# The rest of a block (merge, recurrence, outputs) asked for two steps later within the next block

## The chip, the cores and the metric

The kernel runs on one core of a Trainium2 chip. The metric is the device time of one execution in microseconds (us). The core's engines are TensorE (PE, with its weight loads PEld), VectorE (DVE), ScalarE (ACT), GpSimd (POOL) and SyncE (SP, which here issues the DMAs). Each engine works through a queue of its own in order, and the engines wait for each other by semaphores.

## The reference

One inference step of a hybrid layer over 4096 prompt rows and 32 sample rows of width 1024:

```
h    = RMSNorm_pre(x);  proj = h @ w_in
y_a  = B_a * conv3(C_a * X_a) * silu(Z_a)                  # group A, 512 channels
q,k,v = silu(conv4(qkv)); q,k L2-normalised                # group B, 4 heads x 128
S_t  = exp(g_t) (I - beta_t k_t k_t^T) S_{t-1} + beta_t k_t v_t^T ;  o_t = q_t^T S_t / sqrt(128)
y_g  = RMSNorm_head(o) * silu(Z_g)
y    = x + RMSNorm_post(concat(y_a, y_g) @ w_out)
```

The recurrence of group B is computed by chunks: within a chunk a triangular system is inverted, and only the state S goes from chunk to chunk. The kernel takes chunks of 128 rows.

## The kernel before

The work has three stages. Stage 1 does group B for 16 blocks of 256 rows (two chunks each, c = 0 and 1); stage 2 does group A; stage 3 multiplies with w_out and norms. The change lies in stage 1.

Within stage 1 the loop over blocks (L767) goes through eight steps `si` (L746): four pairs of q and k columns, two pairs of v columns, two pairs of gate columns z. Each step multiplies one pair of column tiles with the block (`proj`, L382: 48 matmuls of 128x256 f16, written as hi and lo halves, L388 to L390) and convolves or gates the result. In the built program the result tile of block 7 is `pj7_c4` (first step), then `pj7_c6`, `c0`, `c2`, `c8`, `c10`, `z0`, `z2`. Between the steps stand:

- `xprep` (step 2) and `gates` (step 3) for the block that follows, and `decays` after its last step. `gates` makes small matmuls (tile `ggate`, L286 and L288), a chain of small DVE and ACT operations (L290 to L321) and the sums over it (tile `gcs`, L326 to L330);
- `stage1` (steps 4 and 5, one chunk each; 3 and 4 in the last two blocks): transposes (L426), the products of k with k and q (L442), DVE masks them (L443, L444), SP writes the 32x32 diagonal parts to DRAM (L450);
- `subst` (step 5): SP reads those parts back (L485), DVE scales (L490), and POOL inverts the 32x32 triangles in 62 dependent operations after one larger one (L495, L499, L500); SP writes the result (tile `lt`, L503) and reads it in another layout (tile `Tc`, L510);
- `finish` for the block before (L748), which is what the change touches. Its part 0 is `merge` (L516): from the 32x32 inverses the 128x128 ones, by many matmuls of 32x32 and 64x64 (tile `m`, L546 to L560, the first of which read `Tc`). Part 1 is `rec_a` of chunk 0 (tiles `rt`, `rk`, `rq`, `rv`, `rS`, L574 to L596, ending in the new state S at L599), part 2 is `rec_b` of chunk 0 (tiles `oo` and `om`, L611 to L632) and `rec_a` of chunk 1, part 3 is `rec_b` of chunk 1;
- `prep_a`, at some steps: preparation of the weights of group A (tiles `gL`, `gu`, `hl`).

The written order is not yet the order on the engines. The framework's scheduler (switched on at L1249) puts each engine's queue in an order of its own: of what stands ready in its model it prefers what was written earlier. The queues are then fixed, and the chip runs each of them in order. The scheduler also has to respect the buffers: M, at and kd (L431, L437) have four buffers for two chunks a block, v and zg two, U (L513) and Tc (L504) one, PSUM bank `m` one, banks `r` two.

After the loop, `finish` is called once more for the last block (L830).

Of the kernel before, what the change touches and what calls it, by code (L numbers as in the profile page):

```python
# [31 lines left out]
BIT = 1 << 23  # L32
NXT = 5
SG = 0
LS = 2
XPE = 256
AH = 1
# [13 lines left out]
def hybrid_kernel(  # L51
# [513 lines left out]
    def rec_a(b, c):  # L565

        C = b["C"]
        nm = f"{b['id']}_{c}"
        sl = slice(c * C, (c + 1) * C)
        qk, v, U, kd = b["qk"], b["v"], b["U"][c], b["kd"][c]  # L570
        S = state[b["s"]]
        vt = bank("r", [P, NH, P], f"t{nm}")[:C]
        for h in range(NH):
            T.transpose(vt[:, h], v[:, h, sl], ident)  # L574
        R = tl([P, NH, P], F32, "R", 2, nm)[:C]
        for h in range(NH):
            A.activation(R[:, h], vt[:, h], AF.Copy, scale=b["br"][:, c, h:h + 1])
        pk = bank("r", [P, NH, P], f"k{nm}")[:C]
        for h in range(NH):
            T.matmul(pk[:, h], qk[:, h, 0, sl], S[:, h], start=True, stop=True)  # L580
        for h in range(NH):
            V.scalar_tensor_tensor(R[:, h], pk[:, h], b["nbe"][:, c, h:h + 1], R[:, h], ALU.mult, ALU.add)
        pq = bank("r", [P, NH, P], f"q{nm}")[:C]
        for h in range(NH):
            T.matmul(pq[:, h], qk[:, h, 1, sl], S[:, h], start=True, stop=True)
        o = tl([P, NH, P], F32, "o", 2, nm)[:C]
        for h in range(NH):
            A.activation(o[:, h], pq[:, h], AF.Copy, scale=b["e1"][:, c, h:h + 1])
        pv = bank("r", [P, NH, P], f"v{nm}")[:C]
        for h in range(NH):  # L590
            T.matmul(pv[:, h], U[:C, h, :C], R[:, h], start=True, stop=True)
        vn = tl([P, NH, P], F32, "vn", 1, nm)[:C]
        A.activation(vn, pv, AF.Copy)
        pS = bank("r", [P, NH, P], f"S{nm}")
        for h in range(NH):
            T.matmul(pS[:, h], kd[:, h], vn[:, h], start=True, stop=True)  # L596
        Sn = tl([P, NH, P], F32, "S", 3, nm)
        for h in range(NH):
            V.scalar_tensor_tensor(Sn[:, h], S[:, h], b["egl"][:, c, h:h + 1], pS[:, h], ALU.mult, ALU.add)  # L599
        state[b["s"]] = Sn  # L600
        b["rec"] = (o, vn)

    def rec_b(b, c):

        C = b["C"]
        nm = f"{b['id']}_{c}"
        sl = slice(c * C, (c + 1) * C)
        o, vn = b["rec"]
        po = bank("o", [P, NH, P], f"o{nm}")[:C]
        for h in range(NH):  # L610
            T.matmul(po[:, h], b["at"][c][:, h, :C], vn[:, h], start=True, stop=True)  # L611
        V.tensor_tensor(o, o, po, ALU.add)
        so = tl([P, 3, NH], F32, "so", 2, nm)[:C]
        jk = b["at"][c]
        for h in range(NH):
            A.activation(jk[:, h], o[:, h], AF.Square, accum_out=so[:, 0, h:h + 1])
        f = so[:, 1]
        V.tensor_tensor(so[:, 0], so[:, 0], b["c2"][:, c], ALU.mult)
        V.tensor_scalar(so[:, 0], so[:, 0], EPS, None, ALU.add)
        rsqrt(so[:, 0], f, so[:, 2])  # L620
        V.tensor_tensor(f, f, b["cc"][:, c], ALU.mult)
        V.tensor_tensor(o, o, bc(f, 2, P), ALU.mult)
        pm = bank("o", [P, NH, P], f"m{nm}")[:, :, :C]
        for h in range(NH):
            T.transpose(pm[:, h], o[:, h], ident[:C, :C])
        mg = b["zg"][:, :, sl]
        V.scalar_tensor_tensor(mg, pm, gwc, mg, ALU.mult, ALU.mult)
        if b["s"]:
            dma(mxd_s[:, NH:], mg)
        else:  # L630
            o0 = b["o"] + c * C
            dma(mxd[o0 // NB2][:, NH:, o0 % NB2:o0 % NB2 + C], mg)  # L632
# [14 lines left out]
    def prep_b(ct):  # L647

        for i, w in enumerate(scaled((ct, ct + 1))):
            hi, lo = W[ct + i] = w_tile(ct + i)  # L650
            A.activation(hi, w, AF.Copy)
            (V if ct + i in VLO else G).tensor_tensor(lo, w, hi, ALU.subtract)  # L652
        if ct < 28:
            c = ct - 16
            V.tensor_tensor(cw[:, :, c:c + 2], cw[:, :, c:c + 2], bc(usc[:, ct:ct + 2], 1, 4), ALU.mult)
# [52 lines left out]
    def out_state(b):  # L708
        dma((ngd_s if b["s"] else ngd_p)[0, 0].rearrange("h k v -> k h v"), state[b["s"]])
# [3 lines left out]
    smp = blocks1[0]  # L713
    groups[SG].insert(0, smp)
    xprep(groups[0][0])
# [6 lines left out]
    prep_b(20)  # L722
    if SG == 0:
        xprep(groups[0][1])
# [22 lines left out]

    def finish(prevs, si):  # L748

        for p in prevs:  # L750
            n = p["nch"]
            if si == 0:
                merge(p)
            elif si == 1:
                rec_a(p, 0)
            elif si == 2:
                rec_b(p, 0)
                if n > 1:
                    rec_a(p, 1)
            elif si == 3:  # L760
                if n > 1:
                    rec_b(p, 1)
                if p["last"]:
                    out_state(p)

    prevs = []
    for gi, grp in enumerate(groups):  # L767
# [11 lines left out]
        for si, (kind, c0) in enumerate(steps):  # L779
# [11 lines left out]
            for b in grp:  # L791
# [5 lines left out]
                else:  # L797
                    h0 = c0 % 4
                    qkv_pair(b, c0, b["qk"][:, h0:h0 + 2, 0 if kind == "k" else 1, :n])
            finish(prevs, si)  # L800
            if si == (2 if gi else 6) and gi + 1 < len(groups):
                for b in groups[gi + 1]:
                    xprep(b)
            s1 = 4 if gi + LS < len(groups) else 3
            if si in (s1, s1 + 1):
# [20 lines left out]
        prevs = grp  # L826
# [1 line left out]
        prep_a()  # L828
    early.close()
    for si in range(4):  # L830
        finish(prevs, si)
    late.close()


# [418 lines left out]
```

## Time and profile before

| | |
|---|---|
| median of 3 runs | 2398.5 us (2389.68 to 2398.57) |
| profiled execution, its own time | 2393.51 us |
| its span, first to last instruction | 2391.8 us |
| mean granted TensorE clock | 0.962 |
| last projection matmul of stage 1 | starts at 1320.27 us |
| PE busy | 2156.4 us, 90% of the span |
| DVE, POOL, ACT busy | 1699.0 (71%), 1195.2 (50%), 992.5 us (41%) |

The span lies 1.7 us below the profiled execution's own time, which lies 5.0 us below the median of the runs. Busy time is the time in which an engine had an instruction of the program in work. Matmuls overlap, so PE's busy share is read together with its idle time and with the granted clock (1.0 is 2.4 GHz, 0.5 is 1.2 GHz; values between are means over both).

### The profile page before, as it was taken

Reading aid. Unit: us, or ns where it says so; the run is one execution under the profiler, and the core shown is the slowest. Engines: PE = TensorE matmul, PEld = TensorE weight load, DVE = VectorE, ACT = ScalarE, POOL = GpSimd, SP = SyncE. Lnnn points to the kernel's source line nnn. Section 1 sums busy time; section 2 is a strip of 40 time slices with the busy share of each in tenths; the row PEclk is TensorE's granted clock in tenths of the full one; section 3 lists DMA queues with packets and bytes.
Section 4 is the critical chain, followed back from the end, with each engine's and each line's share of the span. In section 5 each row is a group of like instructions: output and inputs, shape, how many; then the busy total and the mean of one; then the engine's idle time right before and its main releaser. Section 6 shows DMA issues by size and latency. Waiting matters only on the chain. (4 is left out here: it accounts for less than half of the span.)

```text
span 2391.8 us, 48652 instructions
## 1 busy us (share of the span) xinstructions
PE 2156.4 (90%) x18626; PEld 1706.8 (71%) x18626; DVE 1699.0 (71%) x4666; ACT 992.5 (41%) x2497; POOL 1195.2 (50%) x1581
## 2 busy tenths in 40 slices
PE   3677989899999999999999799899999999999998
PEld 3566877778777777787778678788888887444443
DVE  4886878987689888786777675676575565666763
ACT  4454656565666566555654220222121121433321
POOL 3526246752575644454454740766456611554542
PEclk9888999999999999999989899999999999999999
DMA  6334333534333442244324304311211133443431
GB/s 117 53 93 106 80 75 96 116 82 92 92 100 78 109 112 75 68 91 118 70 72 125 101 24 174 104 66 54 80 59 39 54 100 98 136 150 115 157 115 54
DMA packets 296913, 221.39 MB, mean 93 GB/s; under 512 B 166392, under 2 KB 236856, under 8 KB 296680
## 3 DMA queue, kind: packets, MB, share of 16 engines
q1 hardware_dynamic: 296680, 218.28, 33.5%
q8 instruction: 146, 2.39, 0.4%
q14 instruction: 87, 0.71, 0.1%
HBM read 127.84 MB, written 74.64 MB: 85 GB/s over the span
## 5 line engine op out<-in xcount | busy, mean ns | idle before, releaser
L388 PE MATMUL pj_c<-hhi,w 128*128 128x256 f16 x1536 | 429.3, 280 | 1.2 <-DMA hhi<-xth 1.2
L390 PE MATMUL pj_c<-hhi,w 128*128 128x256 f16 x1536 | 429.7, 280 | 0.0
L389 PE MATMUL pj_c<-hlo,w 128*128 128x256 f16 x1536 | 428.9, 279 | 0.0
L867 PEld LDWEIGHTS <-w_a 128*128 128x128 f16 x2880 | 269.9, 99 | 59.5 <-issue 25.6
L1130 PEld LDWEIGHTS <-opm 128*128 128x128 f16 x1536 | 149.6, 98 | 189.8 <-issue 15.5
L500 POOL TENSOR_TENSOR lt<-lt 128x112 f32<-128x112 f32 (+29 forms) x496 | 250.0, 504 | 38.9
L495 POOL TENSOR_TENSOR la<-la,lt 128x1024 f32<-128x1024 f32 x16 | 38.7, 2421 | 449.9 <-DVE lt L490 270.9
L390 PEld LDWEIGHTS <-w 128*128 128x128 f16 x2176 | 215.5, 100 | 53.2 <-POOL w L652 23.0
L499 POOL TENSOR_TENSOR lt<-la,lt 128x112 f32<-128x112 f32 (+29 forms) x496 | 233.1, 470 | 38.8
L388 PEld LDWEIGHTS <-w 128*128 128x128 f16 x2176 | 215.8, 100 | 34.1 <-issue 2.1
L389 PEld LDWEIGHTS <-w 128*128 128x128 f16 x2176 | 215.7, 100 | 30.7 <-issue 0.5
L405 DVE SCALAR_TENSOR_TENSOR qk<-u,cw,qk 128x256 f32<-128x256 f32 x384 | 214.9, 596 | 9.0 <-ACT qk L403 8.4
L867 PE MATMUL pja<-op,w_a 128*128 128x256 f16 x1536 | 194.5, 276 | 7.0 <-DVE w L881 3.4
L1079 POOL TENSOR_TENSOR mab<-mab 128x1024 bf16<-128x1024 bf16 (+2 forms) x48 | 103.6, 2159 | 130.8 <-ACT mab L1077 128.4
L867 PE MATMUL ga<-op,w_a 128*128 128x256 f16 x1152 | 149.8, 275 | 14.0 <-DVE w L881 8.1
L389 PE MATMUL pj_z<-hlo,w 128*128 128x256 f16 x512 | 144.6, 282 | 0.0
L390 PE MATMUL pj_z<-hhi,w 128*128 128x256 f16 x512 | 144.4, 282 | 0.0
L388 PE MATMUL pj_z<-hhi,w 128*128 128x256 f16 x512 | 144.3, 282 | 0.0
L1130 PE MATMUL pjo<-w_o,opm 128*128 128x512 f16 x528 | 118.2, 379 | 3.8 <-DVE v13y L1154 2.0
L1130 PE MATMUL ro<-w_o,opm 128*128 128x512 f16 x504 | 114.7, 383 | 3.9 <-DVE v7y L1154 2.0
L881 DVE TENSOR_TENSOR w<-pja,w 128x256 f32<-128x256 f32 x168 | 67.4, 420 | 70.6 <-PE pja L867 68.0
L1130 PE MATMUL go<-w_o,opm 128*128 128x512 f16 x504 | 112.7, 379 | 3.9 <-DVE v19y L1154 2.0
(707 smaller groups left out, 4946.5 us busy)
## 6 DMA issues: line engine op xcount, KB each, us to landing
xt<-in_x_prompt_dram SPq DMA_DIRECT2D x32, 512.0 KB
op<-hTd SPq DMA_DIRECT2D x32, 512.0 KB
mx<-mxd SPq DMA_DIRECT2D x16, 1024.0 KB
xtw<-in_w_in_dram SPq DMA_DIRECT2D x28, 512.0 KB
wad<-hl SPq DMA_DIRECT2D x56, 256.0 KB
gB<-gd SPq DMA_DIRECT2D x16, 516.0 KB
hTd<-hhi SPq DMA_DIRECT2D x16, 512.0 KB
hTd<-hlo SPq DMA_DIRECT2D x16, 512.0 KB
```

Source lines behind the costliest of these rows:

```text
L388: T.matmul(pt[:, i, :n], wh[:, k, :], b["hi"][:, k, :n], start=k == 0, stop=False)
L389: T.matmul(pt[:, i, :n], wh[:, k, :], b["lo"][:, k, :n], start=False, stop=False)
L390: T.matmul(pt[:, i, :n], wl[:, k, :], b["hi"][:, k, :n], start=False, stop=k == KT - 1)
L405: V.scalar_tensor_tensor(d, u[:, i, j:j + n], cw[:, j, c0 + i:c0 + i + 1], d, ALU.mult, ALU.add)
L495: E.tensor_tensor(la, la, bc(rl, 1, 32), ALU.mult)
L499: E.tensor_tensor(tm, bc(la[:, j, j + 1:32], 2, w), bc(lt[:, j, 0:w], 1, r), ALU.mult)
L500: last = E.tensor_tensor(lt[:, j + 1:32, 0:w], lt[:, j + 1:32, 0:w], tm, ALU.subtract)
L867: T.matmul(out, lt(x, k), rh(y, k), start=start and k == n == 0, stop=stop and k == 3 and n == 2)
L881: V.tensor_tensor(dst, p, src, ALU.add)
L1079: G.tensor_tensor(ab[:, 0:m], ab[:, 0:m], ab[:, m:2 * m], ALU.add)
L1130: T.matmul(p, mo[:, x, k, t * P:t * P + m], WO[y, k][:, hf * 512:hf * 512 + 512], start=k == i == 0, stop=k == KT - 1 and i == 2)
```

## The change

`finish` subtracts FS = 2 from the step, so that its parts 0 to 3 are asked for at steps 2 to 5 instead of 0 to 3; at the other steps it does nothing. The call after the loop adds 2 again, so that the last block ends as it did.

```diff
 SG = 0
+FS = 2
 LS = 2
...
     def finish(prevs, si):
 
+        si -= FS
         for p in prevs:
             n = p["nch"]
             if si == 0:
                 merge(p)
...
     for si in range(4):
-        finish(prevs, si)
+        finish(prevs, si + FS)
     late.close()
```

Both programs hold the same instructions, as many of each line on each engine; only their order differs. Line numbers of the new program are one higher from L35 on and two higher from L751 on. Three places follow.

PE, where the merge of block 6 starts. Before, this is in the last projection of block 7 (`pj7_z2`):

```order
L388 MATMUL pj7_z2_9716<-hhi7_8033,w30_31_1930 128x256
L389 LDWEIGHTS w30_31_1930
L389 MATMUL pj7_z2_9716<-hlo7_8034,w30_31_1930 128x256
L546 MATMUL m6_8771<-Tc6_8542,M6_0_8328 32x32
L625 MATMUL om5_1_8154<-ident_63,o5_1_8011 128x128 x4
L546 MATMUL m6_8771<-Tc6_8542,M6_0_8328 32x32
L390 LDWEIGHTS w31_31_1931
L390 MATMUL pj7_z2_9716<-hhi7_8033,w31_31_1931 128x256
```

Now it is in `pj7_c10`, two projections earlier, and the gate sums of block 8 (`gcs8`) and the last transposes of block 5 (`om5_1`) stand right in front of it:

```order
L330 LDWEIGHTS g38_9188
L330 MATMUL gcs8_9193<-ctr_76,g38_9188 8x129
L626 MATMUL om5_1_8399<-ident_63,o5_1_8252 128x128 x4
L547 MATMUL m6_8895<-Tc6_8542,M6_0_8295 32x32
L331 MATMUL gcs8_9193<-ident_63,beta8_9181 8x128
L547 MATMUL m6_8895<-Tc6_8542,M6_0_8295 32x32
L427 MATMUL gt07_0_9358<-ident_63,qk7_8698 128x128 x4
L547 MATMUL m6_8895<-Tc6_8542,M6_0_8295 32x32
L389 LDWEIGHTS w20_26_1454
L389 MATMUL pj7_c10_9394<-hhi7_7908,w20_26_1454 128x256
```

So the merge, asked for two steps later in the program, stands earlier in PE's queue than before. From the last product of `stage1` of a block (L442) to the first merge multiply of that block (L546) the queue holds these projection matmuls, by block:

| block | 3 | 4 | 5 | 6 | 7 | 8 | 9 | 10 | 11 | 12 | 13 |
|---|---|---|---|---|---|---|---|---|---|---|---|
| before | 284 | 289 | 328 | 318 | 294 | 284 | 289 | 288 | 328 | 315 | 296 |
| now | 282 | 282 | 288 | 279 | 280 | 289 | 279 | 280 | 289 | 279 | 279 |

Before, the merges of blocks 3, 4, 8, 9 and 10 start in the `c10` projection of the block that follows, those of 5, 6, 7, 11, 12 and 13 in `z0` or `z2`; now all eleven start in `c10`.

DVE, the start of the chain of the gates of block 8. Before, the convolution of block 7 (L405) and an output of block 5 (L627) stand between its links:

```order
L290 COPY g168_9277<-ggate8_9244 128x32
L292 TENSOR_TENSOR gz8_9279<-g168_9277 128x16
L400 COPY hist7_8701<-u7_8_9377 128x6
L293 TENSOR_TENSOR gz8_9279<-gz8_9279,ug_97 128x16
L294 TENSOR_TENSOR gz8_9279<-gz8_9279,dtb_94 128x2x4
L297 TENSOR_SCALAR gex8_9283<-gz8_9279 128x2x4
L405 SCALAR_TENSOR_TENSOR v7_8699<-u7_8_9377,cw_98,v7_8699 128x256
L296 SCALAR_TENSOR_TENSOR gex8_9283<-gz8_9279 128x2x4
L405 SCALAR_TENSOR_TENSOR v7_8699<-u7_8_9377,cw_98,v7_8699 128x256 x2
L302 TENSOR_SCALAR gu8_9287<-gex8_9283 128x16
L405 SCALAR_TENSOR_TENSOR v7_8699<-u7_8_9377,cw_98,v7_8699 128x256
L627 SCALAR_TENSOR_TENSOR zg5_6597<-om5_0_7980,gwc_95,zg5_6597 128x4x128
```

Now the small operations of block 5's last norm (`so5_1`) stand there:

```order
L291 COPY g168_9165<-ggate8_9132 128x32
L399 COPY u7_10_9443<-hist6_7650 128x2x3
L293 TENSOR_TENSOR gz8_9167<-g168_9165 128x16
L294 TENSOR_TENSOR gz8_9167<-gz8_9167,ug_97 128x16
L619 TENSOR_TENSOR so5_1_8379<-so5_1_8379,sm5_7405 128x4
L295 TENSOR_TENSOR gz8_9167<-gz8_9167,dtb_94 128x2x4
L298 TENSOR_SCALAR gex8_9171<-gz8_9167 128x2x4
L620 TENSOR_SCALAR so5_1_8379<-so5_1_8379 128x4
L297 SCALAR_TENSOR_TENSOR gex8_9171<-gz8_9167 128x2x4
L115 TENSOR_SCALAR so5_1_8379<-so5_1_8379 128x4
L116 TENSOR_SCALAR so5_1_8379<-so5_1_8379 128x4
L303 TENSOR_SCALAR gu8_9175<-gex8_9171 128x16
```

The two chains, of the gates and of the norm, now run side by side, and no large operation lies within them there.

SP, where the inverses of block 7 are stored and read back. Before, an output of block 6 (L632) and the gate rows of block 9 (L340, L342) are issued ahead of them:

```order
L632 DMA mxd3_112<-zg6_7649 128x4x128
L340 DMA gd9_10370<-row9_10366 8x129
L342 DMA bd9_10372<-brow9_10368 8x128
L503 DMA ltd7_9623<-lt7_9547 128x256
L510 DMA Tc7_9625<-ltd7_9623 128x4x8 x8
L450 DMA lad8_9786<-M8_0_10462 32x4x32 x4
```

Now the second output of block 6 and the gate rows come behind them:

```order
L504 DMA ltd7_9623<-lt7_9547 128x256
L511 DMA Tc7_9625<-ltd7_9623 128x4x8 x8
L633 DMA mxd3_112<-zg6_7649 128x4x128
L341 DMA gd9_10258<-row9_10254 8x129
L343 DMA bd9_10260<-brow9_10256 8x128
L451 DMA lad8_9786<-M8_0_10429 32x4x32 x4
```

So here the store and the load that feed the merge stand ahead of the DMAs that wait for DVE's gate rows and for the output of block 6.

## Rows read from the trace of the kernel before

**Rows 1.** The page: span, busy time, PE's busy tenths and clock by slices.
```profile
span 2391.8 us, 48652 instructions
PE 2156.4 (90%) x18626; PEld 1706.8 (71%) x18626; DVE 1699.0 (71%) x4666; ACT 992.5 (41%) x2497; POOL 1195.2 (50%) x1581
...
PE   3677989899999999999999799899999999999998
...
PEclk9888999999999999999989899999999999999999
```

**Rows 2.** Timeline of PE, two projection matmuls: start, duration, instruction.
```profile
854.76 0.27 PE L390 MATMUL pj_z<-hhi,w 128*128 128x256 f16 x1
854.87 0.27 PE L388 MATMUL pj_z<-hhi,w 128*128 128x256 f16 x1
```

**Rows 3.** Windows: stretch, length, busy by engine (x), PEclk, DMA share, GB/s.
```profile
407.20:1248.60 841.40, 777.41 (x7226) 658.79 (x7224) 679.46 (x2068) 492.63 (x1316) 457.63 (x825) 0.96 0.37 90
...
563.20:634.60 71.40, 65.41 (x617) 56.44 (x615) 53.71 (x177) 40.77 (x107) 46.22 (x79) 1.00 0.46 108
...
863.50:943.80 80.30, 73.11 (x663) 60.89 (x661) 69.58 (x189) 46.51 (x123) 48.34 (x79) 0.94 0.42 97
...
1019.50:1095.50 76.00, 69.46 (x618) 58.29 (x616) 53.91 (x177) 40.80 (x107) 46.22 (x79) 0.93 0.45 107
1095.50:1170.70 75.20, 69.20 (x651) 59.41 (x649) 61.95 (x197) 46.12 (x126) 34.35 (x68) 1.00 0.30 70
```

**Rows 4.** Waits of PE from 407.2 to 1248.6: total us, times, longest.
```profile
PE m L546 <- DMA Tc<-ltd: 18.5, 12, 2.4
PE rk L580 <- DVE S L599: 9.3, 10, 3.0
PE om L625 <- DVE o L622: 7.8, 11, 1.4
PE gu L206 <- DVE wu L199: 7.1, 4, 2.3
PE gcs L326 <- DVE g L321: 6.8, 5, 2.6
```

**Rows 5.** Windows of two, three, three and three blocks.
```profile
407.20:563.20 156.00, 143.06 (x1333) 120.56 (x1332) 126.60 (x367) 91.83 (x243) 81.32 (x147) 0.96 0.37 84
563.20:786.90 223.70, 207.08 (x1964) 178.12 (x1962) 181.15 (x587) 134.68 (x359) 127.05 (x226) 0.99 0.40 99
786.90:1019.50 232.60, 215.23 (x1996) 180.67 (x1993) 191.78 (x548) 135.38 (x362) 125.87 (x226) 0.95 0.37 90
1019.50:1248.60 229.10, 212.04 (x1942) 179.45 (x1939) 179.94 (x568) 130.73 (x353) 123.38 (x226) 0.95 0.35 85
```

**Rows 6.** Timeline of PE: rS of chunk 0 and rk of chunk 1, block 6.
```profile
738.07 1.06 PE L596 MATMUL rS<-vn,kd 128*128 128x128 f32 x8
...
744.31 0.91 PE L580 MATMUL rk<-S,qk 128*128 128x128 f32 x3 [2.98 <-DVE S L599]
```

**Rows 7.** Timeline of PE: last gate matmul for block 8, its first gate sum.
```profile
678.32 0.34 PE L288 MATMUL ggate<-wg,hlo 128*128 128x8 f16 x8
...
689.11 0.18 PE L326 MATMUL gcs<-g,rev 128*128 128x24 bf16 x1
```

**Rows 8.** Timeline of POOL: first and last operation of the inversions of blocks 12, 13.
```profile
1118.80 2.54 POOL L495 TENSOR_TENSOR la<-la,lt 128x1024 f32<-128x1024 f32 x1 [29.65 <-DVE lt L490]
...
1157.06 0.21 POOL L500 TENSOR_TENSOR lt<-lt 128x8 f32<-128x8 f32 x1
...
1187.60 2.47 POOL L495 TENSOR_TENSOR la<-la,lt 128x1024 f32<-128x1024 f32 x1 [27.57 <-DVE lt L490]
...
1221.02 0.20 POOL L500 TENSOR_TENSOR lt<-lt 128x8 f32<-128x8 f32 x1
```

**Rows 9.** Timeline of PE: the first merge multiply of blocks 12 and 13.
```profile
1160.99 0.24 PE L546 MATMUL m<-Tc,M 32*32 32x32 f32 x2 [1.57 <-DMA Tc<-ltd]
...
1225.03 0.24 PE L546 MATMUL m<-Tc,M 32*32 32x32 f32 x2 [1.77 <-DMA Tc<-ltd]
```

## The prediction, made before the changed kernel was run

> **What bounds the kernel now.** I read the page first [rows 1]. The reader is to see that PE is busy for 90% of a span of 2391.8 us and that its row is at 9 tenths in most slices after the start: PE sets the time. The change lies in stage 1, whose projections end at about 1320 us. A projection matmul starts 0.11 us after the one before it [rows 2], and each block has 8 x 48 = 384 of them, 42 us; with its smaller matmuls a block takes 71 to 80 us [rows 3].
>
> Next come the windows. I take the eleven blocks of the steady state, 4 to 14, from 407.2 to 1248.6 us: each holds the merge and the recurrence of the block before it, 3 to 13. They take 841.4 us, in which PE is idle for 841.4 - 777.4 = 64.0 us at a mean granted clock of 0.96 [rows 3]. If PE is what everything waits for, a clock of 0.96 loses 4% of the stretch, some 34 us. So idle time and clock together, about 98 us, are all that another order of the same work can win here, and there is as much room for a loss.
>
> Last, the list of PE's waits in this stretch [rows 4]. The largest is the merge waiting for Tc: 18.5 us in 12 waits. No wait is longer than 3 us. The rest of a block is late in none of these rows by anything like a step (some 9 us): PE has filled the time with projections already.
>
> **The change, part by part.** It adds and removes no instruction, so the work costs nothing more. What moves is the order, and less of it than two steps: the scheduler had already put the merge where Tc lands in its model, five or more steps into the next block. Asked for later, it now stands in c10 in all eleven blocks, where five of the eleven stood already. Six merges (blocks 5, 6, 7, 11, 12, 13) come one or two projections earlier.
>
> *The wait for Tc, and idle time as a whole.* The old queue has both places, so it prices them itself. Three late merges (5, 6, 7) lie in 563.2 to 786.9: idle 223.70 - 207.08 = 16.6 us. Three early ones (8, 9, 10) in 786.9 to 1019.5: idle 232.60 - 215.23 = 17.4 us. Three late ones again (11, 12, 13) in 1019.5 to 1248.6: 17.1 us [rows 5]. Early against the mean of late: +0.5 us for three, **+1 us** for six. The merge is not earlier than its data allow, because POOL's inversion, which it waits for, hangs on stage1 and not on finish, and its queue keeps its order. From the last product of stage1 to the merge the new queue has 279 to 289 projections; of the early merges before, 284 to 289. So Tc should be waited for as those were, about 2 us each.
>
> *The clock.* The same windows show 0.99 and 0.95 with the late merges, mean 0.97, and 0.95 with the early ones, on a nearly equal number of matmuls (1964, 1942 and 1996) [rows 5]. 0.02 of 229 us is 4.6 us for three merges, 9 us for six. But the windows 563.2 to 634.6 and 1019.5 to 1095.5 hold a queue that repeats after six blocks (617 and 618 matmuls), one at 1.00 in 71.4 us, the other at 0.93 in 76.0 us [rows 3]: the clock moves by as much without a change of order. I take half, **+5 us**, with bounds of 0 and +9.
>
> At this place the Trainium skill speaks against the change: "TensorE: Matmul & The Clock Gate", section "A second HAM failure mode: psum-queue depth-cycling", tells of a kernel whose PE idles briefly and often between groups of matmuls, so that its clock swings between the two levels and throughput goes to that. The trace agrees in kind: no wait here is longer than 3.0 us, and the clock is below 1.0 in every stretch all the same. By the rule alone every merge placed among short waits would be paid for; the sum by it is that of the third rival, 2415 us, against 2402 by the rows.
>
> *The recurrence.* In block 6 rk of chunk 1 stood 4 projections and 18 small gate matmuls behind rS of chunk 0, and waited 2.98 us for the state [rows 6]; in the new queue 18 projections, 2 us, lie between. That wait should go: **-3 us**. The other rk waits (9.3 us in all with this one, [rows 4]) keep their distance of some 19 projections or get more; lower bound -6, upper 0.
>
> *Gates and the last transposes.* These now stand in a row directly ahead of the merge. From the last gate matmul to the first gate sum took 689.11 - 678.66 = 10.4 us in block 7, where PE did not wait for it [rows 7]; the new queue has 69 to 76 projections there, 7.5 to 8.3 us. So PE will come to gcs about 2 us early in each block. I price this at **0**, because the merge right behind it would wait about as long for Tc anyhow: two waits that end at the same time cost one. Without that cover it would be 2.1 us in eleven blocks, 23 us. Bounds 0 and +23.
>
> *The queues of SP and POOL.* On SP the store and load of the inverses go past an output DMA and the gate rows in some blocks. The load starts no earlier for it where POOL is the one waited for: from the end of POOL's last operation to the merge it takes 1160.99 - 1157.27 = 3.7 us in block 12 and 1225.03 - 1221.22 = 3.8 us in block 13 [rows 8, 9], one store and one load with nothing left to take out. The gate rows now wait behind them, but are read only after the block's last step. Cost 0. M, at and kd have four buffers, which hold two blocks; the last part of finish is over before stage1 takes the third: no new wait. The end of stage 1 and the stages behind it keep their order but for a few matmuls: 0.
>
> Sum: 2393.5 us of the profiled execution + 1 + 5 - 3 + 0 = 2396.5 us. The median of the runs lies 5.0 us above that execution, so I forecast **2402 us**, +0.1%. No change that can be measured; about 0.5% (12 us) is what a measurement of this kernel can tell from none.
>
> **The rivals.**
>
> *Faster: Tc arrives before PE does.* POOL's 63 operations took 1157.27 - 1118.80 = 38.5 us in block 12 and 1221.22 - 1187.60 = 33.6 us in block 13 [rows 8], the same operations beside other DVE work. If the new neighbours leave them at 33.6 us everywhere, Tc lands up to 4.9 us earlier, the 18.5 us of waits go [rows 4], and with them perhaps half of the 34 us of clock: -35 us, 2363 us. For it: DVE's large operations lie elsewhere now. Against: block 13 with its 33.6 us still waited 1.77 us [rows 9], and the place of the merge follows the same model.
>
> *Slower: the gate chain becomes the wait that ends last.* It decides from the point where gcs is ready later than Tc. Price 2.1 us in eleven blocks, +23 us: 2422 us with the forecast's other terms near zero. For it: the new distance of 7.5 to 8.3 us lies below the 10.4 us that the chain took in block 7. Against: Tc's wait stands in the same place and covers it.
>
> *Slower: the clock falls at every merge.* The rule of the Trainium skill quoted above, in "TensorE: Matmul & The Clock Gate", points this way. The worst early block ran at 0.94 [rows 3]; eleven blocks at 0.94 instead of 0.96 give 0.02 x 841.4 = +17 us, 2415 us. For it: the two stretches with early merges are at 0.96 and 0.95 [rows 5]. Against: a late one is at 0.95 too, and its worst block at 0.93.
>
> **How the numbers follow.** The forecast 0.54, the faster rival 0.18, the gate chain 0.13, the clock 0.15. The forecast's own range takes the bounds of its terms, -5 to +10 us on the median, 2394 to 2409, and half of the runs' scatter of 9 us to either side: 2389 to 2413. The whole range reaches up past both slower rivals, to 2426, and down into the milder third of the faster one, 2380; below that I leave 0.12, above 0.07. Slower by over 0.5%: 0.13 + 0.15 = 0.28; faster 0.18; within, 0.54.
>
> **What would show it.** In the changed profile: equal counts of instructions; from 407 to 1249 us about the same length of eleven blocks (840 to 850 us); PE idle of 60 to 68 us; waits of m for Tc of 15 to 22 us, gcs up, the rk wait of 3 us gone; a clock of 0.95 to 0.96. The forecast is wrong if the idle time of the stretch moves by more than 10 us or its clock by more than 0.015, and then the line that moved tells which rival came: m with POOL's duration, gcs, or the clock alone.

## The result, and the profile after

The changed kernel takes 2419.92 us (median of 4 runs, 2417.8 to 2426.01), the kernel before 2394.09 us in the same measurement (4 runs, 2389.16 to 2398.57). The ratio is 1.0115, with a 95% interval of 1.0091 to 1.0139: slower by about 26 us. That lies inside the whole range of the prediction (2380 to 2426), but above the forecast's own (2389 to 2413), and on the side of the two slower rivals. The forecast itself, 2402 us and no change that can be measured, missed.

The page of the changed kernel, and the window of the blocks 4 to 14, which now run from 405.5 to 1270.2 us (stretch, length, busy by engine, PEclk, DMA share, GB/s), answer to [rows 1, 3]:

```profile
span 2416.1 us, 48665 instructions
...
PE 2164.4 (90%) x18626; PEld 1713.7 (71%) x18626; DVE 1723.5 (71%) x4666; ACT 990.7 (41%) x2497; POOL 1201.4 (50%) x1581
```
```profile
405.50:1270.20 864.70, 786.68 (x7274) 664.26 (x7273) 698.97 (x2069) 492.58 (x1319) 461.78 (x825) 0.95 0.36 88
```

The reader is to see three things. The eleven blocks take 864.7 us instead of 841.4, so 23.3 of the 24.3 us by which the two profiled spans differ were lost here; the stretch starts 1.7 us earlier than before, and nothing behind stage 1 moved by more than a few us. PE's idle time in it is 864.7 - 786.7 = 78.0 us instead of 64.0. And DVE is busy for 699.0 us instead of 679.5 with one instruction more in the window, and over the whole span for 1723.5 instead of 1699.0 us with 4666 in both: the same work, longer.

PE's waits in this stretch (us in total, times, longest) answer to [rows 4]:

```profile
PE gcs L327 <- DVE g L322: 21.3, 10, 4.9
PE rk L581 <- DVE S L600: 13.2, 11, 2.4
PE rS L597 <- ACT vn L594: 11.2, 9, 1.4
PE om L626 <- DVE o L623: 10.7, 13, 2.3
PE m L547 <- DMA Tc<-ltd: 8.1, 7, 2.8
PE gu L207 <- DVE wu L200: 6.1, 4, 1.7
```

Two further lines of the same view of the kernel before, which did not stand among its rows:

```profile
PE rS L596 <- ACT vn L593: 4.8, 6, 1.2
PE rv L591 <- DVE R L582: 3.9, 5, 1.4
```

The merge's wait for Tc fell from 18.5 to 8.1 us, the wait of the gate sums rose from 6.8 to 21.3, and the waits of the recurrence and the last transposes rose too: rk by 3.9, rS by 6.4, om by 2.9 us; rv's 3.9 us are gone.

The largest single wait shows how it comes. PE at the gate sums in block 7 (start, duration, instruction, idle before it and what ended it; the first line is the last group of gate matmuls), answering to [rows 7]:

```profile
679.68 0.34 PE L289 MATMUL ggate<-wg,hlo 128*128 128x8 f16 x8
...
692.51 0.18 PE L327 MATMUL gcs<-g,rev 128*128 128x24 bf16 x1 [4.94 <-DVE g L322]
```

From the first line to the gate sums 12.8 us pass, 4.94 of them idle. DVE, in the last part of the gate chain at that time:

```profile
686.96 1.08 DVE L312 TENSOR_TENSOR gu<-gu,ru 128x8 f32<-128x8 f32 x1
687.97 0.15 DVE L118 TENSOR_TENSOR so<-so 128x4 f32<-128x4 f32 x1
688.08 1.08 DVE L313 TENSOR_TENSOR gsp<-gsp,gu 128x8 f32<-128x8 f32 x1
689.08 0.15 DVE L119 SCALAR_TENSOR_TENSOR so<-so 128x4 f32<-128x4 f32 x1
689.19 0.17 DVE L314 SCALAR_TENSOR_TENSOR gsp<-gz,gsp 128x8 f32<-128x8 f32 x1
689.27 0.15 DVE L120 SCALAR_TENSOR_TENSOR so<-so 128x4 f32<-128x4 f32 x1
689.39 1.24 DVE L315 TENSOR_TENSOR gsp<-gsp,nea 128x8 f32<-128x8 f32 x1
...
691.28 1.18 DVE L322 TENSOR_TENSOR g<-gsp,g 128x8 bf16<-128x8 f32 x1
```

and POOL, which has finished the inversion and prepares weights of group A:

```profile
685.75 3.39 POOL L676 TENSOR_TENSOR hl<-xtw,hl 128x512 f16<-128x512 f32 x3
689.08 0.31 POOL L492 MEMSET lt<- 128x256 f32 x1
689.35 1.26 POOL L682 TENSOR_TENSOR xtw<-xtw 128x512 f32<-128x512 f32 x1
690.55 0.53 POOL L494 MEMSET lt<- 32x8 f32 x4
691.15 1.28 POOL L684 TENSOR_TENSOR xtw<-xtw,xtw 128x512 f32<-128x512 f32 x1
```

Operations on 8 numbers per partition take 0.15 to 0.17 us, or 1.08 to 1.24 us. The long ones started while POOL ran a 128x512 operation, and ended with it: L315 at 689.39 + 1.24 = 690.63, POOL's L682 at 689.35 + 1.26 = 690.61; L322 at 692.46, POOL's L684 at 692.43. L314, beside POOL's MEMSET, took 0.17. Four such operations make the chain some 4 us longer. In block 8 POOL has no such work at this place, and from the gate matmuls to the gate sums 771.66 - 762.88 = 8.8 us pass:

```profile
762.88 0.34 PE L289 MATMUL ggate<-wg,hlo 128*128 128x8 f16 x8
771.66 0.17 PE L327 MATMUL gcs<-g,rev 128*128 128x24 bf16 x1 [0.77 <-DVE g L322]
```

Over the stretch, the waits of gcs are 1.8 to 4.9 us in the six blocks 4, 6, 7, 9, 10 and 12, where POOL's wide operations lie in the chain, 18.0 us together, and 0.7 to 1.1 us in blocks 5, 8, 11 and 13, where they do not. From the gate matmuls to the gate sums it takes 12.7 to 13.6 us in the six, 8.7 to 8.9 us in the four. Such long operations were no rarer in the gate chains before (22 in the eleven blocks, 23 now). But then PE's queue held 8.7 to 14.6 us of work between the last gate matmul and the first gate sum in the blocks 4 to 13; now it holds 7.5 to 8.7 in the blocks 5 to 13 (an estimate: the operations in between by the order, each at its mean duration in the trace).

### The profile page after: what moved, and what is told of

It reads as the page before. It is cut to its first block, busy times and chain, and to the rows that moved or that the text cites. A ratio compares the mean times of both kernels' runs of the same rounds, so it can differ in the third digit from the quotient of the medians.

```text
span 2416.1 us, 48665 instructions
## 1 busy us (share of the span) xinstructions
PE 2164.4 (90%) x18626; PEld 1713.7 (71%) x18626; DVE 1723.5 (71%) x4666; ACT 990.7 (41%) x2497; POOL 1201.4 (50%) x1581
## 5 line engine op out<-in xcount | busy, mean ns | idle before, releaser
L496 POOL TENSOR_TENSOR la<-la,lt 128x1024 f32<-128x1024 f32 x16 | 38.1, 2380 | 452.3 <-DVE xss L118 281.9
L406 DVE SCALAR_TENSOR_TENSOR qk<-u,cw,qk 128x256 f32<-128x256 f32 x384 | 203.8, 569 | 11.1 <-ACT qk L404 10.3
L898 ACT ACTIVATE op<-tsc 128x512 f16<-128x512 f32 x60 | 37.8, 629 | 191.5 <-POOL tsc L904 116.4
```

Of the source, the lines that this page charges most:

```text
L406: V.scalar_tensor_tensor(d, u[:, i, j:j + n], cw[:, j, c0 + i:c0 + i + 1], d, ALU.mult, ALU.add)
L496: E.tensor_tensor(la, la, bc(rl, 1, 32), ALU.mult)
L898: A.activation(f[:, q, 0, hf], t, AF.Copy)
```

## The experiments

Three theories stood first. *Gate theory*: the loss is the short distance between gate matmuls and gate sums. *Place theory*: merges that all lie in c10 cost by themselves, by short waits and the clock. *Priority theory*: what counts is which parts of `finish` the scheduler sees behind which neighbour. In the built queues, asking later for the last outputs alone (part 3 at step 4 or 5) changes nothing at all; the order of the kernel before comes out again. All times below are medians of the runs of that measurement, with the ratio to the kernel before in it.

**Only the recurrence later** (merge asked for at step 0, rec_a of chunk 0 and the part behind it at step 3, the last outputs at 5).

```diff
+    FIN = (0, 3, 3, 5)   # steps of parts 0 to 3; before: (0, 1, 2, 3)
...
```

(`finish` then does part k at step FIN[k]; that code is left out here.)

> Parts 0 to 3 of finish at steps 0, 3, 3, 5: of the whole change only the first recurrence (part 1) passes xprep; the merge and the outputs stand where they did before gates. In its queue the merge of blocks 3 to 13 starts in c10 in every block, as in the changed kernel, and 69 to 77 projections lie between the last gate matmul and the first gate sum, 7.5 to 8.4 us, as in the changed kernel. Gate theory (PE comes to the gate sum before DVE has finished its chain, pays, and the clock falls behind it): as slow as the changed kernel, 2410 to 2422 us, gcs waits of 18 us or more in all. Place theory (the merge in c10 costs, by its neighbours and the clock): the same time, gcs waits of any size. Priority theory (what costs is that outputs and second recurrence come behind the gates): as before, 2390 to 2400 us.

Measured: 2415.41 us, ratio 1.0082 (1.0052 to 1.0112). Most of the loss, with the merge asked for where it was, and the gate sums wait for 18.9 us: as the gate theory and the place theory expected. The priority theory's 2390 to 2400 us are missed.

**The rest behind the gates** (merge and first recurrence asked for as before, the parts behind them after the gates).

```diff
+    FIN = (0, 1, 4, 5)
...
```

> Parts at steps 0, 1, 4, 5: only the second recurrence and the outputs pass the gates. In its queue every merge of blocks 3 to 13 still starts in c10 or just behind it, but 8 to 14 us of projections (mean 10.5) lie between the last gate matmul and the first gate sum, with 8.4 to 15.6 us before the last transposes. Gate theory: near the kernel before, 2393 to 2406 us, gcs waits of 12 us or less. Place theory: as slow as the changed kernel, 2412 to 2422 us, clock 0.957 or less. Priority theory: as slow as the changed kernel.

Measured: 2432.18 us, ratio 1.0145 (1.011 to 1.0181). Its distance from gates to gate sums is 7.8 to 14.3 us, mostly longer than in the changed kernel, and it is slower. The gate theory's 2393 to 2406 us are missed, and its gate sums wait for 15.7 us where 12 at most were expected. The other two theories have the direction, but too small a loss.

**Gates one step earlier** (in the changed kernel).

```diff
-            if si == (3 if gi else 7) and gi + 1 < len(groups):
+            if si == (2 if gi else 7) and gi + 1 < len(groups):
```

> The changed kernel (FS = 2) with the gates of the block that follows asked for at step 2 instead of 3. In its queue every merge starts in c10 and even 2 us earlier than in the changed kernel, but 9.4 to 14.3 us of projections lie between the last gate matmul and the first gate sum. Gate theory: the loss goes, 2390 to 2402 us, gcs waits of 9 us or less. Place theory: the loss stays, 2412 to 2422 us, clock 0.957 or less. Priority theory: as slow as the changed kernel.

Measured: 2436.41 us, ratio 1.0172 (1.0142 to 1.0203), with a distance of 9.4 to 14.3 us. The slowest of all, where the gate theory expected the loss to go; the gate sums still wait for 14.9 us. Its gate chains have only 5 operations of over 0.9 us from block 4 to 14, against 22 in the kernel before and 23 in the changed one, but the norm's (tile `so`) have 21, against 6 and 2, and PE waits for om for 15.3 us.

**Three steps later instead of two.**

```diff
-FS = 2
+FS = 3
```

> FS = 3. Every merge in c10; 9.3 to 15.7 us of projections before the gate sums, 9 to 11 us before the last transposes. Gate theory: between the two kernels, 2395 to 2408 us, gcs waits of 6 to 14 us. Place theory: 2412 to 2422 us. Priority theory: as slow as the changed kernel or slower.

Measured: 2425.14 us, ratio 1.0124 (1.0095 to 1.0153). The distance is 9.3 to 15.7 us and the gate sums wait for 0.7 us in all, but now the last transposes wait. PE's waits in its blocks 4 to 14:

```profile
PE om L626 <- DVE o L623: 21.3, 10, 3.9
PE m L547 <- DMA Tc<-ltd: 14.4, 10, 3.2
```

The wait of om is again one for a chain of small DVE operations (the norm). So the gate theory fell in its narrow form: the distance of the gates is one of several, and lengthening it moved the wait to another chain. In the two longest of these waits (3.9 us) operations of the gate chain that take 1.1 to 1.2 us stand among those of the norm; in others (3.3 us at 917.48 us) it is the convolution (L406) that stands there. The *contention theory* came out of the first kind: these chains are long where POOL's 128x512 operations run, and PE waits for whichever of them is tight in the queue. Of the four runs only the first speaks against the priority theory, which says nothing of how the time is lost.

**POOL's 128x512 operations left out**, in the old and the new places, with a copy by ACT for the missing half.

```diff
-            G.tensor_tensor(hl[:, 1], src, hl[:, 0], ALU.subtract)
+            A.activation(hl[:, 1], src, AF.Copy)
...
-        G.tensor_tensor(a22, a21, a22, ALU.add)
```

(The other three sums and differences went likewise; the old places are FS = 0.)

> The kernel before, with one part left out: in the preparation of group A's weights, the 128x512 operations of POOL (the low half of each split, and the four sums and differences ahead of it). A copy by ACT takes the place of the low half, so that the DMAs and tiles stay; the weights of group A are then wrong. Contention theory (what the change costs is that the gate chain and the norm chain now lie where POOL runs these operations, beside which small DVE operations take 1.1 instead of 0.16 us): here the gain is small, 2383 to 2394 us, since six of the eleven merges and their chains lie elsewhere. Place theory (a merge in the c10 projection costs by itself, whatever POOL does): 2385 to 2400 us. This run is the base for the next one.

> The changed kernel with the same part left out (POOL's 128x512 operations in the preparation of group A's weights, a copy by ACT in place of the low half). Its queue still has all eleven merges in c10. Contention theory: the small DVE operations of the gate chain are back at 0.16 us, the chain takes 8.5 us in every block, the idle time of PE from block 4 to 14 is 60 to 68 us, and this kernel lies at most 8 us above the same one with the old places (no_pool_prep_before). Place theory: it lies 18 to 30 us above it, as the changed kernel lies above the one before, with idle time still at 75 us or more.

Measured: 2402.85 us with the old places, ratio 1.0034 (1.0014 to 1.0054), and 2404.48 us with the new, 1.0042 (1.0022 to 1.0062): the change now costs 1.6 us instead of 26. No DVE operation of the gate chains took over 0.9 us in either. But the first number missed its range, the idle time of the second is 79.6 us where 60 to 68 were expected, and its gate sums still waited for 14.1 us. From block 4 to 14 of the second, ACT waits for 33.5 us, once for 15.8, until a DMA has stored an earlier part of the weights and freed its buffer (hl has four); in these blocks of the kernel before and of the changed one it never waits for that. What stands behind it in ACT's queue is late, gates and recurrence too, which made this pair a poor test.

**The preparation asked for later**, behind the gate chain of the next block, all work kept, in the old and the new places.

```diff
-            if si == 6 and 1 <= gi <= 13 or si == 2 and gi in (4, 7, 10):
+            if si == 4 and 2 <= gi <= 14:
...
+                        tc.issue_after(groups[gi + 1][-1]["gates_end"]):
```

> The kernel before, all work kept: the preparation of group A's weights is asked for in step 4 of the next block and issued only behind that block's gate chain, so that POOL's 128x512 operations no longer lie beside the gates. Contention theory: gate chain 8.5 us in every block, 2380 to 2394 us. Place theory: no difference from the kernel before, 2390 to 2400 us.

> The same move of the preparation in the changed kernel; it too puts POOL's 128x512 operations behind the gate chain, and the queue then has the merges partly in c10 and partly in z0 (their places change with it). Contention theory: gate chain 8.5 us in every block, idle time 60 to 68 us from block 4 to 14, 2388 to 2402 us. Place theory: the blocks whose merge stays in c10 stay slow, 2405 to 2420 us.

Measured: 2427.05 us, ratio 1.0136 (1.0109 to 1.0163), and 2426.19 us, 1.0138 (1.0104 to 1.0172). Both theories missed. The gate chains had no slow operation any more except in block 14, but POOL's operations now ran beside other ones: in the first kernel PE waited 14.3 us for om and 5.9 us for kd. So PE waited elsewhere instead.

**POOL's operations left out, nothing put in their place** (the DMA stores the high half twice).

```diff
-            G.tensor_tensor(hl[:, 1], src, hl[:, 0], ALU.subtract)
-            dma(wad[i][:, k], hl)
+            dma(wad[i][:, k], bc(hl[:, 0], 1, 2))
...
```

(The four sums and differences went as above.)

> The changed kernel, with POOL's 128x512 operations in the preparation of group A's weights left out, and this time nothing put on ACT in their place: the DMA stores the high half twice. The weights of group A are then wrong. PE's queue keeps the distances of the changed kernel: 7.5 to 8.6 us of work between the last gate matmul and the first gate sum, and every merge in c10. Contention theory: the gate chain is at most 9.5 us long in every block instead of 12.4 to 13.4 us in six of them, the waits of gcs fall from 21.3 to at most 9 us from block 4 to 14, the idle time from 78 to 62 to 70 us, and the time is 2398 to 2410 us. Queue theory (the chain is long because of the other DVE work that stands in it): the gcs waits stay at 17 us or more, and the time at 2412 to 2422 us.

> The same part left out (POOL's 128x512 operations in the preparation of group A's weights, nothing put in their place) with the old places of merge, recurrence and outputs: the partner of the run that took the changed kernel from 1.0115 to 1.0014 of the kernel before. Contention theory (most of what the change costs comes from chains of small DVE operations that now lie beside these operations): without them the old and the new places differ by at most 8 us, so a ratio of 0.998 to 1.005 to the kernel before, 2391 to 2408 us. Place theory (the new places cost about 25 us whatever POOL does, and leaving POOL's work out is worth 21 us in either kernel): a ratio of 0.988 to 0.993, 2367 to 2379 us.

Measured: with the new places 2398.48 us, ratio 1.0014 (0.9995 to 1.0033); with the old 2397.26 us, ratio 1.0007 (0.9991 to 1.0024). So the same removal takes 1.0% off the changed kernel and, on balance, nothing off the kernel before, and without these operations the two places can't be told apart. That is what the contention theory said, and the place theory's 0.988 to 0.993 for the second did not come. The gate chain of block 7 in the first of the two, from the last group of gate matmuls to the gate sums, and one of its operations on DVE, with no wait left:

```profile
690.99 0.34 PE L289 MATMUL ggate<-wg,hlo 128*128 128x8 f16 x8
698.73 0.18 PE L327 MATMUL gcs<-g,rev 128*128 128x24 bf16 x1
```
```profile
697.12 0.17 DVE L315 TENSOR_TENSOR gsp<-gsp,nea 128x8 f32<-128x8 f32 x1
```

7.7 us instead of 12.8, with the same operations, and 0.17 us instead of 1.24. PE's waits in its blocks 4 to 14:

```profile
PE m L547 <- DMA Tc<-ltd: 22.1, 10, 11.7
PE rS L597 <- ACT vn L594: 14.8, 6, 9.8
PE gu L207 <- DVE wu L200: 12.8, 7, 2.3
PE rk L581 <- DVE S L600: 12.3, 7, 7.8
...
PE gcs L327 <- DVE g L322: 1.0, 1, 1.0
```

The wait of gcs went from 21.3 to 1.0 us, as expected; the idle time did not fall to 62 to 70 us, it is 79.4. But 29.4 us of it are three single waits, of m (11.7), rS (9.8) and rk (7.8), longer than any in these blocks of the changed kernel. The last two stand behind ACT, which waits again until a buffer of the weights is free, 20.4 us in all; at rS:

```profile
ACT hl L675 <- DMA wad<-hl: 20.4, 7, 9.1
```
```profile
911.96 0.63 ACT L675 ACTIVATE hl<-xtw 128x512 f16<-128x512 f32 x1 [8.69 <-DMA wad<-hl]
912.50 0.58 ACT L594 ACTIVATE vn<-rv 128x512 f32<-128x512 f32 x1
```

The products rv that this vn reads had ended at 899.9 us. The wait of 11.7 us for Tc at 461.5 us, where the store of the inverses took some 10 us, stands in its partner too (11.64 us at 457.7) and in the kernel with ACT's copies and the old places (11.75 us at 453.1), while no wait for Tc in these blocks is longer than 6.1 us in the ten kernels that keep POOL's operations. So the removal brings waits of its own. Without the three, 50.0 us of idle time are left, and the waits are 10.4 us for m, 5.0 for rS and 4.5 for rk.

**The scaling ahead of the inversion on DVE**, in the old and the new places, all work kept: the one other wide operation of POOL in a block, 128x1024 and 2.4 us.

```diff
-        E.tensor_tensor(la, la, bc(rl, 1, 32), ALU.mult)
+        V.tensor_tensor(la, la, bc(rl, 1, 32), ALU.mult)
```

> The kernel before, all work kept: the 128x1024 multiplication at the head of the inversion, 2.4 us on POOL in each block, is done by DVE. Contention theory, in its strong form (the time that DVE loses beside POOL is what PE waits for): DVE gains more than it gives, about 23 us less lost from block 4 to 14 against some 12 us of work added, and POOL's chain is shorter, so 2375 to 2392 us. Theory of the lucky order (every order other than that of the kernel before costs 8 to 42 us by waits that turn up on other lines, as in all eight other orders so far): 2400 to 2425 us, although DVE loses less.

> The same move of the 128x1024 multiplication to DVE in the changed kernel. Contention theory in its strong form: 2392 to 2410 us. Theory of the lucky order: 2405 to 2430 us, within 8 us of the run with the old places (scaling_on_dve_before), since neither is then the order of the kernel before.

Measured: 2426.92 us, ratio 1.0131 (1.0096 to 1.0166), and 2419.51 us, 1.009 (1.0066 to 1.0113). The contention theory in its strong form fell. Its premise did not hold in the first kernel: DVE is busy for 692.5 us there from block 4 to 14, 13.0 more than before, as much as the work added (11 operations of 1.22 us). In the second it is busy for 691.6, 7.4 less than in the changed kernel, and the time is not clearly below that of the changed kernel (1.009 against 1.0115, with intervals that overlap). The theory of the lucky order has the second and misses the first by 2 us. The first kernel's merges wait for Tc for 37.4 us:

```profile
PE m L547 <- DMA Tc<-ltd: 37.4, 11, 6.1
```

In its queue most merges stand 42 to 44 us of PE's work (an estimate as above) behind the last product of stage1, against 44 to 51 us in the kernel before: it seems that the scheduler counts on an earlier Tc and places them earlier than it comes. No version that keeps all the work beat the kernel before.

**All runs by one account.** Blocks 4 to 14 of each profiled run: length, idle time of PE (length less busy), what the clock took (for each of the eleven blocks its length times 1 less its PEclk, summed), and the rest.

| | ratio | length | idle | clock | rest |
|---|---|---|---|---|---|
| before | 1 | 841.4 | 64.0 | 32.5 | 744.9 |
| changed | 1.0115 | 864.7 | 78.0 | 39.9 | 746.8 |
| only the recurrence later | 1.0082 | 866.5 | 76.3 | 44.0 | 746.2 |
| rest behind the gates | 1.0145 | 879.5 | 91.4 | 42.8 | 745.3 |
| gates one step earlier | 1.0172 | 886.9 | 94.2 | 47.0 | 745.6 |
| three steps later | 1.0124 | 862.2 | 73.9 | 41.8 | 746.5 |
| preparation later, old / new places | 1.0136 / 1.0138 | 857.7 / 855.9 | 76.1 / 76.6 | 36.1 / 35.9 | 745.5 / 743.3 |
| ACT copy, old / new places | 1.0034 / 1.0042 | 852.3 / 861.2 | 75.6 / 79.6 | 35.6 / 40.1 | 741.1 / 741.4 |
| left out, old / new places | 1.0007 / 1.0014 | 849.2 / 855.6 | 76.9 / 79.4 | 31.7 / 34.3 | 740.7 / 741.9 |
| scaling on DVE, old / new places | 1.0131 / 1.009 | 867.5 / 866.6 | 82.3 / 72.2 | 47.6 / 57.5 | 737.6 / 736.9 |

The rest is the same within 3.5 us in the first eight kernels. PE has the same work in all fourteen, though, and in the last six kernels the rest is 3 to 8 us lower than before: the account closes to some 8 us, not better. (PEclk has two digits, which alone leaves one or two us open in the clock column.) So a new order changes mainly the first two columns, as the prediction had it, and in all thirteen other kernels the idle time is longer than before.

## Why the prediction was right or wrong

**What bounds the kernel: right.** The account above is the prediction's own (idle time and clock), and it closes: +14.0 idle, +7.4 clock, +1.9 rest make the 23.3 us. Its frame, some 98 us of idle time and clock to be won and as much room for a loss, was right; the change lost.

**Merges in c10, work unchanged: right.** Equal counts of instructions, and POOL's inversion took as long as before: its two repeating lines add up to 331.7 us (line, engine, operation, count; busy us, mean ns; idle before), and in the kernel before to 330.3. So the faster rival, an earlier Tc, did not come: the 33.6 us of block 13 in [rows 8] were not to be had everywhere.

```profile
L501 POOL TENSOR_TENSOR lt<-lt 128x112 f32<-128x112 f32 (+29 forms) x341 | 166.4, 488 | 26.7
L500 POOL TENSOR_TENSOR lt<-la,lt 128x112 f32<-128x112 f32 (+29 forms) x341 | 165.3, 485 | 26.7
```
```profile
L500 POOL TENSOR_TENSOR lt<-lt 128x112 f32<-128x112 f32 (+29 forms) x341 | 166.3, 488 | 26.7
L499 POOL TENSOR_TENSOR lt<-la,lt 128x112 f32<-128x112 f32 (+29 forms) x341 | 164.0, 481 | 26.7
```

**Idle time: the step that failed.** The prediction wrote "The old queue has both places, so it prices them itself", +1 us. It measured +14.0: +4.1 us at the gates and the merge together, +2.9 at om, +6.4 in the recurrence (rk and rS less rv). The place of the merge was not the only thing that changed: in the old early blocks the gate chain and the norm chain stood apart from the merge with other distances, so their idle time of 17.4 us in three blocks [rows 5] was no price for the new order. A window prices a place together with its neighbours.

The whole range held the result, the forecast's own did not. That own range takes "the bounds of its terms" as -5 to +10 us, but the term of the gates has a bound of +23, which it leaves out. The 5.0 us added for the median were scatter of three runs: in the measurement beside the changed kernel the median lies 0.6 us above the profiled execution.

**Gates and last transposes at 0: half right, for the reason given.** The wait of gcs did rise, by 14.5 us, and the merge's wait behind it fell by 10.4: most of it was one wait under another name, and the pair rose by 4.1 us. When the gate chain was shortened by experiment, though, the merge's wait did not take its place: without the one wait of 11.7 us it is 10.4 us, against 8.1. But the 2.1 us per block were read from block 7 [rows 7], where none of POOL's wide operations lie in the chain. That was not the length of the chain everywhere. Counted from the start of the last group of gate matmuls it was 689.11 - 678.32 = 10.8 us there, with convolutions between its links; now it is 8.7 to 8.9 us where DVE is free of POOL's wide operations, so PE waits for 0.7 to 1.1 us there and not for 2.1, and 12.7 to 13.6 us where it isn't, against 7.5 to 8.7 us of queue. And om, counted as covered with it, had no cover: +2.9 us. Its three longest waits, 2.3 us each in blocks 6, 9 and 12, come behind two operations of the gate chain that take 1.17 and 1.08 us.

**The recurrence, -3 us: wrong in sign.** The wait of 2.98 us in block 6 [rows 6] went as said; rk of chunk 1 there follows without any:

```profile
753.88 1.16 PE L597 MATMUL rS<-vn,kd 128*128 128x128 f32 x8 [1.07 <-ACT vn L594]
759.74 1.16 PE L581 MATMUL rk<-S,qk 128*128 128x128 f32 x8
```

But rk as a whole rose by 3.9 us and rS by 6.4, in many waits of 1.0 to 1.5 us; only rv's 3.9 us went. One block's wait was taken as a term, and its neighbours' as constant. The trace shows what stands right ahead of them: other work on DVE and ACT, not an operation held up by POOL's 128x512 ones. In eight of the eleven waits of rk (11.3 of the 13.2 us) DVE has the scaling of the next block's rows (`xth`, L260) ahead of the update of S, which `finish`, asked for later, now follows; before, in two of ten (2.5 of 9.3 us). In all nine waits of rS, ACT has vn right behind an activation (L407) that waits for the convolution on DVE; before, in all six, which are shorter. DVE, ACT and the products of PE that waited, in block 6:

```profile
655.84 1.60 DVE L260 SCALAR_TENSOR_TENSOR xth<-xt,xss,xth 128x1024 f16<-128x1024 f32 x1
...
657.92 1.11 DVE L600 SCALAR_TENSOR_TENSOR S<-S,E,rS 128x128 f32<-128x128 f32 x4
```
```profile
659.09 0.38 PE L581 MATMUL rk<-S,qk 128*128 128x128 f32 x1 [1.46 <-DVE S L600]
```
```profile
669.67 0.63 ACT L407 ACTIVATE qk<-qk 128x512 f32<-128x512 f32 x1 [4.19 <-DVE qk L406]
670.21 0.58 ACT L594 ACTIVATE vn<-rv 128x512 f32<-128x512 f32 x1
```
```profile
670.84 0.38 PE L597 MATMUL rS<-vn,kd 128*128 128x128 f32 x1 [1.42 <-ACT vn L594]
```

So asking for the recurrence behind the preparation of the next rows can have a cost of its own on DVE, but how large it is isn't shown: with POOL's operations left out `xth` stands just ahead of S as often (10 of 22 updates; 11 in the changed kernel, 5 before), and rk waits less.

**The clock, +5 us with bounds of 0 and +9: right in size**, +7.4. All orders of the table that keep the work and wait longer than before also lose more to the clock; for each us of added idle time the changed kernel lost another half. The rule of the Trainium skill ("TensorE: Matmul & The Clock Gate", section "A second HAM failure mode: psum-queue depth-cycling") has brief idling take the clock down; by that the trace agrees, since the granted clock of the stretch fell here from 0.96 to 0.95, with waits of at most 4.9 us. The rival built on it asked for 17 us and got 7.4. Whether the clock follows the idle time is not shown: in the new places of the table's last row it takes 25.0 us more than before, beside 8.2 us more of idle time. Two readings of the prediction need mending: the clock was not below 1.0 in every stretch (two of [rows 3] stand at 1.00), and the worst block with a late merge ran not at 0.93 but at 0.91 (block 14).

**The rivals.** The sum of +26 us is nearest to the gate chain's (+23), by its mechanism only in part: its wait stepped in front of Tc's, as its condition said, but it replaced most of that one, and three others joined. That its price came so near is luck: the pair of waits that it priced rose by 4.1 us, and the rest of the 26 us came from the recurrence, om and the clock. What the rival had not seen is why the chain is late in six blocks, POOL beside DVE.

**How far the cause is shown.** Two things are measured. In the changed kernel's own trace, POOL's 128x512 operations make the gate chain some 4 us longer in six blocks, and 18.0 of the 21.3 us of gcs waits stand there; without these operations 1.0 us is left. And leaving them out takes about 24 us (roughly 17 to 32, by the two intervals) off the changed kernel, 1.0115 to 1.0014, and on balance nothing off the kernel before, 1 to 1.0007.

That the 24 us are the price of the collisions is argued, not shown. Taking the operations out brings waits of its own, and another order too: ACT has vn right behind L407 in 11 of 22 cases in the changed kernel, in 3 without the operations. The largest part of the added idle time in the changed kernel, 6.4 us in the recurrence, stands behind other work on DVE and ACT, an order that no run took away by itself. Nor does the profiled execution show the whole gain: it is the slowest of its ten runs (2405.19 us, median 2398.48), its span is 13.4 us shorter (2416.1 - 2402.7), and of the 9.1 us in blocks 4 to 14 none is idle time (+1.4, with the three long waits of 29.4 us in it; clock -5.6, rest -4.9). And the number of small DVE operations (at most 16 numbers per partition) that take over 0.9 us does not tell the kernels apart: from block 4 to 14 it is 33 in the kernel before, 38 in the changed one and 39 in the slowest; what counts is where they lie, if they do it. So how much of the loss each of the two has, the collisions and the order on DVE and ACT, stays open. In the thirteen other kernels the loss was between 2 and 41 us (0.0007 and 0.0172 of 2395): that the queue of the kernel before suits its waits better than its neighbours do is what the runs agree with, not what one of them proves.

## What to carry to other kernels

Where a scheduler writes the queues, asking for work later can put it earlier, and the place of one operation can't be priced from blocks where its neighbours stand otherwise: compare, for each chain that PE waits on, its length with the work that the new queue holds between its ends. Read that length in several blocks, and look at what the other engines run beside it; here it was 8.8 or 12.8 us. Look also for what stands ahead of each operation of the moved part in the queues of the engines that feed PE. When an experiment takes work out, ask what that work had been holding back. And leave room for the clock: here a us of new idle time came with half a us more lost to it, in the other kernels of the table that keep the work with 0.3 to 3.

## What the runs showed of the hardware

A DVE operation with two inputs of 2 to 8 numbers per partition, 0.15 to 0.17 us long, takes 1.08 to 1.24 us when it starts while POOL runs a 128x512 operation that reads, and ends within 0.04 us of POOL's where the rows above show the end (L313, L315, L322); beside POOL's 128x1024 multiplication at the head of the inversion it takes as long as that does. A row of the norm of the next rows on DVE, and POOL's at that time:

```profile
647.75 0.15 DVE L118 TENSOR_TENSOR xss<-xss 128x2 f32<-128x2 f32 x1
647.94 2.35 DVE L119 SCALAR_TENSOR_TENSOR xss<-xss 128x2 f32<-128x2 f32 x1
650.33 0.16 DVE L120 SCALAR_TENSOR_TENSOR xss<-xss 128x2 f32<-128x2 f32 x1
```
```profile
647.92 2.36 POOL L496 TENSOR_TENSOR la<-la,lt 128x1024 f32<-128x1024 f32 x1 [22.04 <-DVE xss L118]
```

Beside POOL's MEMSET they keep 0.17 us (L314), and without POOL's 128x512 operations as well (L315 in the kernel without them). DVE's busy time in blocks 4 to 14 went from 699.0 to 650.3 us when the changed kernel lost the 77 operations of POOL:

```profile
401.80:1257.40 855.60, 776.16 (x7273) 662.47 (x7272) 650.34 (x2073) 492.75 (x1319) 362.21 (x748) 0.96 0.38 89
```

The Trainium skill has the rule, in "SBUF — State Buffer", section "Who interferes with whom": a DVE instruction with two inputs in SBUF and a GpSimd instruction that reads SBUF use one interface, and the one that issues second is blocked until the first has finished; one that only writes does not count. The trace agrees in all three points, with the durations above, for DVE as the second. The prediction looked at POOL only for the time at which Tc comes, and not for what it does to the small operations of DVE that PE waits for.
